# Low parts of the heads' weights made by an accumulating DMA from GpSimd, and weights split three pieces ahead

## The chip, the cores and the metric

The kernel runs on one core of a Trainium2 chip. The metric is the device time of one execution in microseconds: 1679.33 us is the median of three runs of the kernel before (1678.99 to 1681.47). The core's engines are TensorE (PE, with its weight loads PEld), VectorE (DVE), ScalarE (ACT), GpSimd (POOL) and SyncE (SP), which issues most of the transfers.

## What is computed

The reference is one decoder layer with two branches on 512 tokens of width 2048, all in float32: an attention with forgetting gates (8 heads of 128) and an RWKV-7 recurrence (16 heads of 64), each gated, then merged and projected.

```python
h = _rmsnorm(x, norm_gain)
u = h @ w_in
u_fox, u_rwkv, g_a, g_b = _split(u, (FOX_COLS, RWKV_COLS, D_MODEL, D_MODEL))
q, k, v, z_a, f_logit = _split(u_fox, FOX_SIZES)
o_a = _fox_attention(heads(q), heads(k), heads(v), log_f) * jax.nn.silu(z_a)
r, kr, vr, z_b, w_down, a_down = _split(_token_shift(u_rwkv, rwkv_shift_mix), RWKV_SIZES)
...
y = _rwkv7_scan(rh, heads(decay), kh, vh, kk, kk * ah)
o_b = (y + bonus) * jax.nn.silu(z_b)
m = jax.nn.sigmoid(g_a) * (o_a @ w_proj_fox) + jax.nn.sigmoid(g_b) * (o_b @ w_proj_rwkv)
return _rmsnorm(x + m @ w_out, final_norm_gain)
```

Per step, the scan is `S = S * w + sa * b + v * k` with `sa = S @ (-kk)`; the kernel computes it in eight chunks of 64 tokens for each pair of heads.

## The kernel before

**Three products for one.** Every large product is made of three: the activations are held as `hhi` and `hlo`, a high part that TensorE's fp32r format holds exactly and the rest, and each weight tile is split in the same way into `whi` and `wlo`. A product is then hhi·whi + hlo·whi + hhi·wlo, three matmuls of 128x128 by 128x512 into one accumulator (`product`, L295).

**Pieces.** The weights come in pieces of 256 KB: 128 partitions of four blocks of 128 columns, 12 matmuls each; a tile of 128 output columns has four of them (`_0`, `_4`, `_8`, `_12` in the names). `load_raw` (L253) lets SyncE load a piece into one of `RAWS` = 4 raw buffers. `split_pieces` (L271) makes the two parts: ScalarE copies raw to `whi` with rounding (L283) and VectorE subtracts, raw − whi, to `wlo` (L284). `whi` and `wlo` have four buffers each. `next_piece` (L259) is called when the program comes to a piece i: it issues loads up to piece i+4, splits up to piece i+2, and hands out piece i.

**Stages.** First, the norm, the transposes and two small tiles (`wd`, `ad`). Then the heads' tiles in turn: RWKV head pairs 0 and 1 (tiles k, r, z, v), then a FoX head (tiles fq, fk, fv, fz) and a head pair alternately. From about 950 us on, the gates and projections (pieces named g and p) and the product with `w_out` (o, `raw_o`). The matmuls of the heads' own work are gathered between the large products of the tiles that come later.

**A head pair** goes through: *front* (`rwkv_front`, from L510: the decay `tz`, the rate `a`, the key `kn`, the products `EK` and `AR`, the sums of `rkk`), *back* (`rwkv_back`, L629: a triangular system solved by 31 steps `Wt`, `W` on VectorE, then the small products `gp` and `dp` with the copies `GP`, half of them on ScalarE and half on VectorE, L703, and `DT`), *chain* (`rwkv_chain`, L717: in each of eight chunks `z`, its copy `zt`, `sa`, its copy `AV`, `st`, the new state `SV`; ScalarE also makes `pre` for it; each copy is made half by VectorE and half by ScalarE), and the *end* (`yv`, normalisation of `y`, and a GpSimd store `ob_d`, L796). A FoX head ends with a GpSimd store `oa_d` (L859).

**What sets the order.** The order of TensorE and SyncE is the order of the program, which a small planner makes: `clock[0]` adds up the matmuls' estimated times, and a head's next step runs when its due time by the table `LAG` has come. On VectorE, ScalarE and GpSimd a scheduler orders by priority: chain steps stand highest (`HP` = 300, with `HV` = 300), then the splits (`HW` = 150), then the FoX steps (`HF` = 100). Each engine executes its row in order, so a waiting instruction holds up those behind it.

Of the kernel before, what the change touches and what calls it, by code (L numbers as in the profile page):

```python
# [9 lines left out]
F32 = mybir.dt.float32  # L10
F32R = mybir.dt.float32r
AF = mybir.ActivationFunctionType
ALU = mybir.AluOpType
# [43 lines left out]
def hybrid_layer(  # L57
# [7 lines left out]
    V, S, G, PE = nc.vector, nc.scalar, nc.gpsimd, nc.tensor  # L65
# [187 lines left out]
    def load_raw(name, srcs, nk, M):  # L253
        raw = wpool.tile([P, nk, M], F32, tag="raw", bufs=RAWS, name=f"raw_{name}")
        for off, src in srcs:
            nc.sync.dma_start(raw[:, :, off:off + src.shape[1]], src.rearrange("(k p) m -> p k m", p=P))
        return raw

    def next_piece():  # L259


        i = used[0]
        used[0] += 1
        while len(raws) < min(i + (RAWS + 1 if i > 3 else 4), len(pieces)):
            raws.append(load_raw(*pieces[len(raws)]))
        split_pieces(i + (3 if i > 3 else 1))
        got = parts[i]
        parts[i] = None
        return got

    def split_pieces(n):  # L271
        while len(parts) < min(n, len(pieces)):
            j = len(parts)
            name, srcs, nk, M = pieces[j]
            raw = raws[j]
            whi = wpool.tile([P, nk, M], F32R, tag="whi", bufs=4, name=f"whi_{name}")
            wlo = wpool.tile([P, nk, M], F32R, tag="wlo", bufs=4, name=f"wlo_{name}")
            if j < 4:
                G.tensor_copy(whi, raw)
                G.tensor_tensor(wlo, raw, whi.bitcast(F32), ALU.subtract)  # L280
            else:
                with tc.high_priority(offset=HW):
                    S.activation(whi, raw, AF.Copy)  # L283
                    V.tensor_tensor(wlo, raw, whi.bitcast(F32), ALU.subtract)  # L284
            parts.append((whi, wlo))


# [7 lines left out]
    def product(ps, name, hi, lo):  # L295

        M, nk = spec[name]
        for k0 in range(0, nk, HK):
            whi, wlo = next_piece()
            for k in range(HK):  # L300
                kk = k0 + k
                mm(ps[0:M, :], whi[:, k, :], hi(kk), start=(kk == 0), stop=False)
                yield
                mm(ps[0:M, :], whi[:, k, :], lo(kk), start=False, stop=False)
                yield
                mm(ps[0:M, :], wlo[:, k, :], hi(kk), start=False, stop=(kk == nk - 1))
                yield
# [55 lines left out]
    for hf in range(2):  # L363
        t = slice(256 * hf, 256 * hf + 256)
        for j in range(0, KC + AHEAD, 2):
            if j < KC:
                turn(hf, j)
            if hf == 0 and j % 4 == 0 and j < KC:
                wd_w.append(next_piece())
                if j == 0:  # L370
                    for tb in range(2, 4):
                        for h2 in range(2):
                            load_x(nc.sync, tb, h2)
                    load_params()
            if hf == 0 and j in (SQ2, SQ3):
                norm_rows(2 if j == SQ2 else 3)
            if j < AHEAD:
                continue
            for kk in range(j - AHEAD, j - AHEAD + 2):
                whi, wlo = wd_w[kk // 4]  # L380
                mm(ps_wd[0:MW, t], whi[:, kk % 4, :], hhi[:, kk, t], start=(kk == 0), stop=False)
                mm(ps_wd[0:MW, t], whi[:, kk % 4, :], hlo[:, kk, t], start=False, stop=False)
                mm(ps_wd[0:MW, t], wlo[:, kk % 4, :], hhi[:, kk, t], start=False, stop=(kk == KC - 1))
            if hf == 1 and j - AHEAD in (4, 8, 12):
                split_pieces(4 + (j - AHEAD) // 4)
# [643 lines left out]
    for n in range(4):  # L1029
        pss = banks(n)  # L1030
        for kk in range(KC if n < 3 else KC // 2):
            whi, wlo = next_piece()
            if n == 1 and kk % 2 == 0:
                load_late(KC // 2 + kk // 2)
            for t in range(4):
                out_mm(pss[t], t, kk, whi[:, 0, :], wlo[:, 0, :])
        if n == 3:
            break
        for t in range(4):
            residual(pss[t], t, n)  # L1040
# [47 lines left out]
```

## Time and profile before

| | us |
|---|---|
| median of three runs | 1679.33 |
| the profiled execution's own time | 1682.03 |
| its span | 1680.3 |
| TensorE busy | 1632.0 (97%) |
| VectorE busy | 956.2 (57%) |
| ScalarE busy | 712.2 (42%) |
| GpSimd busy | 82.7 (5%) |

Times in the profile are microseconds from the start of the span. A row of the timeline gives an instruction's start, its duration, engine, line, operation and tiles; in brackets the idle time ahead of it on its engine and what ended that. A group row gives the busy time, the mean in nanoseconds of one, and the idle time ahead with its releasers. Transfers issued by GpSimd, `ob_d` for one, stand in GpSimd's row with the time that their issue takes, and are not counted as busy. The waits view adds up, for each engine, how long it waited for what.

### The profile page before, as it was taken

What the parts mean: (1) busy time and instruction counts of PE and PEld (TensorE: products, weight loads), DVE (VectorE), ACT (ScalarE), POOL (GpSimd) and SP (SyncE); (2) the same over time, 40 slices, a digit from 0 to 9 for tenths busy, and PEclk for the clock granted to TensorE, in tenths of its full rate; (3) what the DMA queues carried; (4) which work ended last, traced back from release to release, by engine and by line L of the source; (5) the groups of instructions that cost most, each with busy time, mean ns of one, the idle gap of its engine ahead of it and who ended that gap; (6) DMA issues with size and microseconds to landing.
All of it is one profiled execution on the core that took longest, in us unless ns stands there. A gap on an engine that the chain in (4) does not pass through costs nothing.

```text
span 1680.3 us, 23444 instructions
## 1 busy us (share of the span) xinstructions
PE 1632.0 (97%) x8506; PEld 1333.1 (79%) x8506; DVE 956.2 (57%) x2005; ACT 712.2 (42%) x1455; POOL 82.7 (5%) x149
## 2 busy tenths in 40 slices
PE   6999998989999989999999999999999999999998
PEld 6887876868778868888788787888888888888886
DVE  6469587795976867778768354222234333353432
ACT  7544455373464454554644444222223222243322
POOL 3000000010000000010000000000000000001110
PEclk9999999999999999999999999999999999999999
DMA  5342423333333423424334234335334333343422
GB/s 166 97 105 70 118 67 89 98 80 85 84 85 94 102 76 85 111 66 114 87 90 110 75 107 126 97 98 144 97 98 145 99 96 95 98 157 122 136 84 100
DMA packets 287978, 170.24 MB, mean 101 GB/s; under 512 B 38790, under 2 KB 270830, under 8 KB 287222
## 3 DMA queue, kind: packets, MB, share of 16 engines
q1 hardware_dynamic: 284358, 156.13, 35.2%
q0 software_dynamic: 2064, 9.46, 1.5%
q10 hardware_dynamic: 1440, 3.15, 0.5%
q8 instruction: 67, 1.10, 0.3%
q14 instruction: 49, 0.40, 0.1%
HBM read 158.19 MB, written 10.50 MB: 100 GB/s over the span
## 4 chain that ended last, share of the span: by engine, by line
PE 87%; DVE 8%; ACT 3%; issue 2%; DMA 1%; SPq 0%; POOL 0%; DVEq 0%; ACTq 0%; POOLq 0%
PE u_g L152 21%; PE o L152 10%; PE p L152 10%; PE u_fk L152 5%; PE u_fq L152 5%; PE u_v L152 5%; PE u_fz L152 5%; PE u_fv L152 4%; PE u_r L152 4%; PE u_z L152 4%; PE u_k L152 4%; DVE Wt L499 2%; PE fo L152 1%; DVE W L675 1%; PE sc L152 1%
## 5 line engine op out<-in xcount | busy, mean ns | idle before, releaser
L152 PE MATMUL u_g<-hhi,whi_g 128*128 128x512 f32 x512 | 200.4, 391 | 0.0
L152 PE MATMUL u_g<-hhi,wlo_g 128*128 128x512 f32 x512 | 200.2, 391 | 0.0
L152 PE MATMUL u_g<-hlo,whi_g 128*128 128x512 f32 x512 | 199.6, 390 | 0.0
L284 DVE TENSOR_TENSOR wlo_g<-raw_g,whi_g 128x512 fp32r<-128x512 f32 x128 | 88.3, 690 | 165.2 <-ACT whi_g L283 163.1
L283 ACT ACTIVATE whi_g<-raw_g 128x512 fp32r<-128x512 f32 x128 | 80.8, 632 | 223.3 <-PE u_g L152 115.9
L152 PEld LDWEIGHTS u_g<-hhi,wlo_g 128*128 128x128 f32 x512 | 96.1, 188 | 20.4
L152 PEld LDWEIGHTS u_g<-hlo,whi_g 128*128 128x128 f32 x512 | 96.1, 188 | 20.2
L152 PEld LDWEIGHTS u_g<-hhi,whi_g 128*128 128x128 f32 x512 | 96.1, 188 | 20.0
L499 DVE TENSOR_TENSOR Wt<-W,Lt 128x16 f32<-128x16 f32 (+30 forms) x248 | 102.4, 413 | 5.5
L284 DVE TENSOR_TENSOR wlo_p<-raw_p,whi_p 128x512 fp32r<-128x512 f32 x64 | 44.3, 692 | 102.0 <-ACT whi_p L283 102.0
L152 PE MATMUL p<-ohi,whi_p 128*128 128x512 f32 x256 | 101.2, 395 | 0.1
L152 PE MATMUL p<-olo,whi_p 128*128 128x512 f32 x256 | 100.2, 391 | 0.5 <-DVE olo L929 0.5
L152 PE MATMUL p<-ohi,wlo_p 128*128 128x512 f32 x256 | 100.4, 392 | 0.0
L283 ACT ACTIVATE whi_p<-raw_p 128x512 fp32r<-128x512 f32 x64 | 40.4, 631 | 122.9 <-PE u_g L152 118.8
L152 PE MATMUL o<-whi_o,mhi 128*128 128x512 f32 x224 | 87.3, 390 | 0.1
L152 PE MATMUL o<-whi_o,mlo 128*128 128x512 f32 x224 | 87.2, 389 | 0.0
L152 PE MATMUL o<-wlo_o,mhi 128*128 128x512 f32 x224 | 87.1, 389 | 0.0
L284 DVE TENSOR_TENSOR wlo_o<-raw_o,whi_o 128x512 fp32r<-128x512 f32 x56 | 42.6, 761 | 76.1 <-ACT whi_o L283 75.9
L675 DVE TENSOR_REDUCE W<-Wt 128x8 f32<-128x16 f32 (+30 forms) x248 | 72.1, 291 | 5.0
L283 ACT ACTIVATE whi_o<-raw_o 128x512 fp32r<-128x512 f32 x56 | 35.3, 631 | 83.5 <-PE o L152 78.5
L744 ACT ACTIVATE pre<-SV,E 64x64 f32<-64x64 f32 x112 | 38.6, 345 | 57.3 <-DVE SV L757 56.5
L152 PEld LDWEIGHTS p<-olo,whi_p 128*128 128x128 f32 x256 | 48.0, 188 | 12.6 <-DVE olo L929 2.1
(353 smaller groups left out, 3937.3 us busy)
## 6 DMA issues: line engine op xcount, KB each, us to landing
raw_g<-in_w_in_dram SPq DMA_DIRECT2D x128, 256.0 KB
raw_o<-in_w_out_dram SPq DMA_DIRECT2D x56, 256.0 KB
raw_k<-in_w_in_dram SPq DMA_DIRECT2D x32, 256.0 KB
raw_r<-in_w_in_dram SPq DMA_DIRECT2D x32, 256.0 KB
raw_z<-in_w_in_dram SPq DMA_DIRECT2D x32, 256.0 KB
raw_v<-in_w_in_dram SPq DMA_DIRECT2D x32, 256.0 KB
raw_fq<-in_w_in_dram SPq DMA_DIRECT2D x32, 256.0 KB
raw_fk<-in_w_in_dram SPq DMA_DIRECT2D x32, 256.0 KB
```

The lines of the kernel that those rows point to most:

```text
L152: PE.matmul(out, lhsT=lhsT, rhs=rhs, start=start, stop=stop, **kw)
L283: S.activation(whi, raw, AF.Copy)
L284: V.tensor_tensor(wlo, raw, whi.bitcast(F32), ALU.subtract)
L499: eng.tensor_tensor(o, a, b, op)
L675: V.tensor_reduce(W[:, :, i], tmp[:, :, 0:i + 1], AX.X, ALU.add)
L744: S.activation(pre[hs[q]], SV[hs[q], c, q, :], AF.Copy, scale=E1[hs[q], c, CH:CH + 1])
```

## The change

For all pieces of the heads' tiles (names beginning with k, r, z, v or f; 256 pieces) `wlo` is no longer made by VectorE. ScalarE writes the negated, rounded raw piece into `wlo`, so that this holds −whi, and a DMA issued by GpSimd adds the raw piece onto it in SBUF. `whi` is made by ScalarE as before. The pieces of `wd`, `ad`, `g`, `p` and `o` keep VectorE's subtraction. Besides, from the ninth piece on the splits run up to piece i+3 in place of i+2. The lines behind the change are five higher than before.

```diff
@@ next_piece
-        split_pieces(i + (3 if i > 3 else 1))
+        split_pieces(i + (4 if i > 7 else 3 if i > 3 else 1))
@@ split_pieces
                 with tc.high_priority(offset=HW):
+                    if name[0] in "krzvf":
+
+                        S.activation(wlo, raw, AF.Copy, scale=-1.0)
+                        G.dma_start(wlo.bitcast(F32), raw, accum_op=ALU.add)
                     S.activation(whi, raw, AF.Copy)
-                    V.tensor_tensor(wlo, raw, whi.bitcast(F32), ALU.subtract)
+                    if name[0] not in "krzvf":
+                        V.tensor_tensor(wlo, raw, whi.bitcast(F32), ALU.subtract)
```

The rows of TensorE and SyncE stand in the same order as before. On the others the order changes as follows (in a name, the numbers behind the tile are the head, the chunk or the piece, and a running number of the buffer).

ScalarE in the chain of head pair 0, first two chunks, before and then after; the weights split there are those of tile k of head pair 2:

```order
L740 COPY zt_0_1868<-z_0_0_1866 64x64
L283 ACTIVATE whi_k2_4_1920<-raw_k2_4_1853 128x512
L750 COPY AV_0_1845<-sa_0_0_1889 64x64
L283 ACTIVATE whi_k2_8_1953<-raw_k2_8_1879 128x512
L744 ACTIVATE pre_0_1930<-SV_0_1069,E1_0_483 64x64 x2
L740 COPY zt_0_1927<-z_0_1_1925 64x64
L283 ACTIVATE whi_k2_12_1977<-raw_k2_12_1918 128x512
L750 COPY AV_0_1845<-sa_0_1_1942 64x64
```

```order
L745 COPY zt_0_1921<-z_0_0_1919 64x64
L287 ACTIVATE whi_k2_4_1934<-raw_k2_4_1905 128x512
L285 ACTIVATE wlo_k2_4_1935<-raw_k2_4_1905 128x512
L755 COPY AV_0_1897<-sa_0_0_1943 64x64
L287 ACTIVATE whi_k2_8_1974<-raw_k2_8_1932 128x512
L749 ACTIVATE pre_0_1985<-SV_0_1096,E1_0_483 64x64 x2
L285 ACTIVATE wlo_k2_8_1975<-raw_k2_8_1932 128x512
L745 COPY zt_0_1982<-z_0_1_1980 64x64
L287 ACTIVATE whi_k2_12_2008<-raw_k2_12_1972 128x512
L755 COPY AV_0_1897<-sa_0_1_1997 64x64
L285 ACTIVATE wlo_k2_12_2009<-raw_k2_12_1972 128x512
```

Beside each `whi` there is now a negation to `wlo`, ahead of `AV`, ahead of the second `zt` and behind the second `AV`.

VectorE ahead of the copy `GP` of head pair 2, before and then after; `kn`, `tz`, `EK`, `AR`, `z` and `rkk` belong to the front of head pair 3:

```order
L284 TENSOR_TENSOR wlo_v3_12_3766<-raw_v3_12_3702,whi_v3_12_3765 128x512
L538 SCALAR_TENSOR_TENSOR tz_3_3660<-reset_531,tz_3_3660 128x512
L499 TENSOR_TENSOR EK_3_3665<-EK_3_3665,k_3_3427 128x512
L557 RECIPROCAL kn_3_3676<-kn_3_3676 128x128
L499 TENSOR_TENSOR AR_3_3684<-r_3_3550,E1_1_484 128x8x64
L284 TENSOR_TENSOR wlo_fq2_0_3808<-raw_fq2_0_3725,whi_fq2_0_3807 128x512
L559 SCALAR_TENSOR_TENSOR kn_3_3676<-k_3_3427,par_448,kn_3_3676 128x512
L567 SCALAR_TENSOR_TENSOR rkk_3_3688<-r_3_3550,par_448,EK_3_3665 128x512
L562 SCALAR_TENSOR_TENSOR AR_3_3684<-kn_3_3676,E1_1_484 128x8x64
L465 SCALAR_TENSOR_TENSOR z_3_3720<-u_z3_3554,par1m_452,z_3_3720 128x511
L443 TENSOR_TENSOR rlo_3_3691<-rkk_3_3688,rhi_3_3690 128x512
L703 COPY GP_2_3755<-gp_2_3738 32x256
```

```order
L543 SCALAR_TENSOR_TENSOR tz_3_3758<-reset_531,tz_3_3758 128x512
L562 RECIPROCAL kn_3_3774<-kn_3_3774 128x128
L564 SCALAR_TENSOR_TENSOR kn_3_3774<-k_3_3518,par_448,kn_3_3774 128x512
L504 TENSOR_TENSOR AR_3_3782<-r_3_3645,E1_1_484 128x8x64
L567 SCALAR_TENSOR_TENSOR AR_3_3782<-kn_3_3774,E1_1_484 128x8x64
L504 TENSOR_TENSOR EK_3_3763<-EK_3_3763,k_3_3518 128x512
L470 SCALAR_TENSOR_TENSOR z_3_3819<-u_z3_3649,par1m_452,z_3_3819 128x511
L572 SCALAR_TENSOR_TENSOR rkk_3_3786<-r_3_3645,par_448,EK_3_3763 128x512
L708 COPY GP_2_3855<-gp_2_3838 32x256
L504 TENSOR_TENSOR BK_3_4003<-EK_3_3763 64x8x64
L448 TENSOR_TENSOR rlo_3_3789<-rkk_3_3786,rhi_3_3788 128x512
```

The subtractions (a third, `wlo_v3_8`, stands directly ahead of the rows shown of before) are gone, and `rlo` stands behind `GP`.

GpSimd around the store `ob_d` of head pair 2, before and then after; `a` and `kn` belong to the front of head pair 4:

```order
L730 COPY AV_3_4809<-SV_3_3975 64x8x64 x2
L796 DMA ob_d_559<-y_2_4435 128x512
L549 TENSOR_SCALAR a_4_4883<-a_4_4883 128x512
L499 TENSOR_TENSOR kn_4_4888<-kn_4_4888,a_4_4883 128x512
L859 DMA oa_d_558<-fz_2_3889 128x512
```

```order
L286 DMA wlo_k4_12_4611<-raw_k4_12_4580 128x512
L286 DMA wlo_r4_0_4638<-raw_r4_0_4608 128x512
L801 DMA ob_d_559<-y_2_4552 128x512
L286 DMA wlo_r4_4_4686<-raw_r4_4_4635 128x512
L286 DMA wlo_r4_8_4711<-raw_r4_8_4683 128x512
L286 DMA wlo_r4_12_4735<-raw_r4_12_4708 128x512
L286 DMA wlo_z4_0_4769<-raw_z4_0_4732 128x512
```

The transfers of the pieces now stand in GpSimd's row ahead of and behind the store, which itself stands between those of `r4_0` and `r4_4`.

## Rows read from the trace of the kernel before

**Rows 1.** The page's head and first part: busy time, share and instructions of each engine.

```profile
span 1680.3 us, 23444 instructions
PE 1632.0 (97%) x8506; PEld 1333.1 (79%) x8506; DVE 956.2 (57%) x2005; ACT 712.2 (42%) x1455; POOL 82.7 (5%) x149
```

**Rows 2.** The page's chain that ended last, share of the span by engine.

```profile
PE 87%; DVE 8%; ACT 3%; issue 2%; DMA 1%; SPq 0%; POOL 0%; DVEq 0%; ACTq 0%; POOLq 0%
```

**Rows 3.** What TensorE waited for: us in total, times, longest.

```profile
PE dp L152 <- DVE GP L703: 9.7, 2, 5.3
...
PE fpt L156 <- ACT tz L536: 4.5, 1, 4.5
PE yv L152 <- DVE ylo L443: 2.6, 4, 0.9
...
PE sa L152 <- ACT zt L740: 1.5, 2, 1.1
```

**Rows 4.** Windows: length; busy PE, PEld, DVE, ACT, POOL; clock; DMA share; GB/s.

```profile
46.00:960.00 914.00, 887.93 (x5118) 721.38 (x5117) 668.26 (x1520) 453.66 (x982) 44.72 (x61) 0.99 0.36 90
240.00:280.00 40.00, 33.51 (x176) 25.13 (x170) 35.82 (x59) 23.23 (x40) 5.27 (x6) 0.91 0.28 75
...
365.50:372.70 7.20, 7.20 (x61) 5.57 (x59) 7.20 (x11) 7.06 (x14) 1.59 (x1) 1.00 0.27 73
...
600.00:640.00 40.00, 36.50 (x219) 30.05 (x220) 24.52 (x50) 16.22 (x44) 1.86 (x2) 0.91 0.23 60
```

**Rows 5.** Groups of VectorE's subtractions from 46 to 990 us.

```profile
L284 DVE TENSOR_TENSOR wlo_fk<-raw_fk,whi_fk 128x512 fp32r<-128x512 f32 x32 | 22.4, 699 | 22.1 <-ACT whi_fk L283 21.9
...
L284 DVE TENSOR_TENSOR wlo_fq<-raw_fq,whi_fq 128x512 fp32r<-128x512 f32 x32 | 21.8, 680 | 11.0 <-ACT whi_fq L283 10.7
```

**Rows 6.** DMA issues by group: count, KB each, median us from issue to landing.

```profile
xo<-in_x_dram POOLq DMA_DIRECT2D x4, 1024.0 KB, 7.4
...
ob_d<-y POOLq DMA_DIRECT2D x8, 256.0 KB, 2.5
```

**Rows 7.** Timeline of TensorE and ScalarE in a stretch at full rate.

```profile
545.46 0.39 PE L152 MATMUL u_fv<-hhi,wlo_fv 128*128 128x512 f32 x1
...
545.66 0.63 ACT L283 ACTIVATE whi_fz<-raw_fz 128x512 fp32r<-128x512 f32 x1 [2.09 <-PE u_fv L152]
...
554.30 0.39 PE L152 MATMUL u_fz<-hhi,wlo_fz 128*128 128x512 f32 x1
```

**Rows 8.** Timeline of VectorE and TensorE, 253 to 260 us.

```profile
253.60 0.63 DVE L284 TENSOR_TENSOR wlo_fq<-raw_fq,whi_fq 128x512 fp32r<-128x512 f32 x1
...
259.29 0.69 PE L156 MATMUL fpt<-ident,pr 128*128 128x128 f32 x4 [4.47 <-ACT tz L536]
259.71 0.71 PE L152 MATMUL u_v<-hhi,wlo_v 128*128 128x512 f32 x1
```

**Rows 9.** Timeline of VectorE and TensorE, 366 to 378 us.

```profile
367.56 1.23 DVE L284 TENSOR_TENSOR wlo_v<-raw_v,whi_v 128x512 fp32r<-128x512 f32 x2
...
372.20 0.67 DVE L284 TENSOR_TENSOR wlo_fq<-raw_fq,whi_fq 128x512 fp32r<-128x512 f32 x1
...
376.28 0.69 DVE L443 TENSOR_TENSOR rlo<-rkk,rhi 128x512 fp32r<-128x512 f32 x1 [0.81 <-POOL kn L499]
...
377.49 0.74 PE L152 MATMUL dp<-DT,GP 32*32 32x32 f32 x20 [4.43 <-DVE GP L703]
```

**Rows 10.** Timeline of GpSimd, and TensorE's first use of `wlo_r4_4`.

```profile
83.73 0.61 POOL L549 TENSOR_SCALAR a<-a 128x512 f32<-128x512 f32 x1 [33.52 <-ACT EK L548]
...
458.93 0.55 POOL L796 DMA_DIRECT2D ob_d<-y  x1 [21.93 <-DVE y L795]
...
462.65 0.39 PE L152 MATMUL u_r<-hhi,wlo_r 128*128 128x512 f32 x1
...
720.81 2.89 POOL L549 TENSOR_SCALAR a<-a 128x512 f32<-128x512 f32 x1 [36.24 <-ACT EK L548]
```

## The prediction, made before the result was known

> **What bounds the kernel now.** I read the page's first part first: TensorE is busy 1632.0 of 1680.3 us, VectorE 956.2, ScalarE 712.2, GpSimd 82.7 [rows 1]. The chain of waits says the same: 87% of the path that ended last is TensorE, 8% VectorE, 3% ScalarE [rows 2]. So the change, which takes no matmul away and adds none, can only act on the 48.3 us in which TensorE stands (1680.3 − 1632.0), and on the clock it is granted. I then read whom TensorE waits for [rows 3]: VectorE's copy `GP` 9.7 us in two waits, ScalarE's `tz` 4.5 in one, VectorE's `ylo` 2.6 in four, ScalarE's `zt` 1.5 in two. No row there names `whi` or `wlo`: the weights' halves are never late, and the subtractions that the change takes away are felt only where other work queues behind them. From 46 to 960 us, where the heads are made, TensorE is busy 887.93 of 914.00 us, so 26.1 us of standing is all that can be had there; VectorE works 668.26 (73%) and ScalarE 453.66 (50%) [rows 4]. The clock is told by the same view: three windows of 40 us, at 240, 360 and 600 us, have a mean granted clock of 0.91, the first and the last shown [rows 4]. Each holds or directly follows one of the three long stalls (4.47, 4.43 and 5.3 us) [rows 3, 8, 9]. At the two levels of 2.4 and 1.2 GHz a mean of 0.91 over 40 us is (1 − 0.91) × 40 / 0.5 = 7.2 us at the lower one, 3.6 us of work lost each time; after the stall at 259 us one matmul of 128x512 takes 0.71 us where 0.39 is usual [rows 7, 8].
>
> **The change part by part.** It concerns 256 pieces (16 tiles' worth of k, r, z, v for eight head pairs and q, k, v, z for eight heads, of four pieces each).
>
> *VectorE loses 256 subtractions.* There are eight groups of about 32; the longest and the shortest mean are 699 and 680 ns [rows 5]. At 0.68 the 256 are 174 us, and VectorE falls from 668 to about 494 of 914 us (54%). What this saves on TensorE's path is read from the stalls one by one.
> Stall A (254.8 to 259.3 us): TensorE waits 4.47 us for `tz`, which ScalarE makes after `y` and `zt`, and `y` waits for a row of reciprocals on VectorE. Three subtractions stand among these (246.75, 251.39 and 253.60 us; the last is shown, 0.63 us) [rows 8]. Up to 1.9 us goes; against this the transpose copy of the turn and the new negations share ScalarE, where one more operation of 0.6 us comes before `tz`: 1.9 − 0.6 = 1.3 (0 to 1.9).
> Stall B (372.8 to 377.5): TensorE waits 4.43 us for `GP`. In VectorE's row before it stand two subtractions (1.23 us) and a third (0.67), 1.9 us; and the new order moves `rlo` behind `GP`, which takes away its 0.69 and the 0.81 that it waited for GpSimd's `kn`, 1.5 us [rows 9]. That is 3.4 us at most. But in this stretch ScalarE is as full as VectorE: 7.06 and 7.20 of 7.20 us [rows 4], and it is given a negation for each of the three pieces that are split there, 3 × 0.63 = 1.9 us [rows 7], while its `tz`, `EK` and `E` feed the same VectorE row. So I count the 1.5 in full, and of the other 1.9 that ScalarE largely pays back a quarter: 2.0 (1.5 to 3.4).
> The third stall (5.3 us, the longest of the `GP` row) has one subtraction ahead of it and one negation in its place: 0 (−0.6 to 0.6). Of the four waits for `ylo` I take half, 1.3 (0 to 2.6).
> Clock: I take it that the most shortened stall, B, falls to some 2.4 us and no longer brings the lower clock: waits of 1.5 us and less [rows 3] have no window of 0.91 about them. 3.6 us (0 to 10.8).
> Gain: 1.3 + 2.0 + 0 + 1.3 + 3.6 = 8.2 us; at most 1.9 + 3.4 + 0.6 + 2.6 + 10.8 = 19.3.
>
> *ScalarE gains 256 activations* of one 128x512 tile, the size of the present `whi` (0.63 us) [rows 7]: 161 us, from 454 to about 615 of 914 us (67%). Two costs. In the chain, the first order fence shows a negation beside each `whi`, between `zt`, `AV` and `pre`; ScalarE copies one half of `zt` and of `AV` in each of 64 chunks, and TensorE waits for both halves; it waited for `zt` only twice, 1.5 us in all [rows 3], so most copies have slack. An activation of 0.63 that happens to run when a copy becomes ready delays it 0.3 us on average; with 161/914 = 18% more occupation and 128 copies that is 128 × 0.18 × 0.3 = 6.9 us of delay, of which I let 1.0 pass (0 to 5). In the fronts, where ScalarE is already full, three or so negations add 1.9 us each; two of eight fronts make TensorE wait today (the `tz` and the `GP` of B) and are counted above; I add one more, 1.9 (0 to 15, rival 1). Cost: 2.9.
>
> *GpSimd gains 256 transfers and TensorE a wait for their landing.* The issue itself takes 0.55 us there [rows 10], 256 × 0.6 = 154 us on an engine that works 44.72 of 914. The order of TensorE and SyncE is row for row the same. What counts is the time from a free slot to the first matmul with that `wlo`. In a stretch at full rate ScalarE begins `whi_fz` at 545.66, released by TensorE, and the first matmul that reads this piece's `wlo` is at 554.30 [rows 7]: 8.64 us, three pieces and a quarter, which is also what the change's look-ahead gives with four buffers. ScalarE needs 2 × 0.63, handing over some 0.2; so 7.1 us are left for issue and landing. The trace holds no transfer from SBUF to SBUF and no accumulating one. The nearest rows are GpSimd's stores of 256 KB, 2.5 us to landing, and its 1024 KB loads, 7.4 [rows 6]. An accumulating one reads twice and writes once, so I take 3 to 5 us, nearer the 256 KB row, and it is hidden; cost 0. At full rate a piece takes 12 × 0.227 = 2.7 us (39 matmuls lie between 545.46 and 554.30 [rows 7]), over the whole stretch 914/260 = 3.5, so most pieces have more time than this one; I take 40 of 256 as at full rate. At the upper bound of 7.4 each of these would be 0.3 us late, 12 us. Queued behind each waiting transfer on GpSimd are the next one, the `a` and `kn` steps and the stores. The `ob_d` store of head pair 2 is issued at 458.93, after a wait for `y`, and the third order fence shows `wlo_r4_4` right behind it; TensorE reads that one from 462.65 on [rows 10], so issue and landing have 462.65 − 459.48 = 3.2 us, just what I take for them. I count 0 for this and for the seven like it (0 to 3).
> The raw buffer is now given back by the landing and not by VectorE, 2 to 4 us later; a 256 KB transfer lands in 2.5 us [rows 6], and the load is issued two pieces, 5.4 us, before ScalarE needs it: 0 (0 to 3).
>
> *What speaks against the landing.* GpSimd's `tensor_scalar` on one shape takes 0.61 us in one place and 2.89 in another, where VectorE is busy too; a store issued from GpSimd beside a busy VectorE takes the usual 0.55 [rows 10]. If the work behind a transfer were held up as that operation was, a landing would be 2.3 us longer, 5.3 to 7.3 us, at its upper end past the 7.1 that are left; this is the greater part of rival 2. The Trainium skill (SBUF — State Buffer, "SBUF: two separate sides") states this rule: a VectorE operation in a two-port mode shuts GpSimd out of the port pair that they share, and a DMA issued there gets its descriptors late. The trace agrees for the compute operation; of transfers no run here shows it yet. By the rule alone the sum would be rival 2's.
>
> *Sum.* 8.2 − 2.9 = 5.3 us. The profiled execution took 1682.03 us, so 1676.7; it lies 2.7 over the median of 1679.33, which gives **1674.0 us**, 0.3% faster. (A measurement of this kernel tells 0.2%, 3.4 us, from no change.)
>
> **The rivals.** *Rival 1, slower: ScalarE becomes the bound of the fronts.* In stretch B it is busy 7.06 of 7.20 us now [rows 4], and I take the fronts of the other pairs to be like it, since they run the same code. If each of the eight is 1.9 us later and no slack is left, that is 15.2, with up to 5 in the chain and one lower-clock spell more (3.6): 23.8 − 8.2 = 15.6 over, 1695; half of it gives 1687. It decides where a front's result has less slack than the three negations ahead of it. For it: A ends on a ScalarE result. Against: only two of eight fronts hold TensorE up, and one of them on VectorE. Chance 0.21.
> *Rival 2, slower: the transfer lands too late,* from 7.1 us on, or GpSimd's queue stands behind `ob_d` and `kn`. At 8.5 us each full-rate piece is 1.4 us late: 40 × 1.4 − 8.2 = 48 us over, 1727; at 7.4, 12 − 5.3 = 7 over, 1686. For it: two reads per write, one queue, and the 2.89 us of [rows 10]. Against: 2.5 us for 256 KB [rows 6]. Chance 0.13.
> *Rival 3, no change:* TensorE's stalls have their own sequence (`kn`, `EK`, reciprocals on a ScalarE as full as VectorE), VectorE's freed time is time that it waits anyway, and the clock falls as before: 8.2 − 3.6 − 2.9 = 1.7 us, 1677.6. Chance 0.20. That the change doesn't do what it says would be this too: VectorE's 256 rows are gone in the new order, so I give that nothing.
> *Forecast,* 1665 to 1675: 0.46.
>
> **How the numbers follow.** Faster 0.46; same 0.20; slower 0.21 + 0.13 = 0.34. The range: below it is bounded by the gain of 19.3 us, 1660; above, half of rival 2 (0.07) and the worst of rival 1 (0.06) are left out, 1698. The forecast's own range is 1664 to 1676.
>
> **What would show it.** In the profile after, VectorE between 46 and 960 us should have about 494 us and ScalarE 615. TensorE's wait for `GP` at 377 should be some 2 us shorter, that for `tz` 1.3, and the window from 360 to 400 us should have a clock of 1.00. A row of TensorE waiting for `wlo`, or for the new transfer, of more than 3 us in all makes the step on the landing wrong; landings over 7 us are rival 2. More waits for `zt`, `tz` or other ScalarE results, over 8 us in all, are rival 1. If the waits shrink but the end doesn't move, the clock term or rival 3 is what failed.

## The result, and the profile after

The changed kernel takes 1689.84 us (median of four runs, 1688.28 to 1690.14) against 1679.45 for the kernel before: a ratio of 1.0058 with a 95% interval of 1.0040 to 1.0075. It is 10.4 us slower, where 5.3 us faster was forecast.

The page after, its first part and the chain [rows 1, 2 are those of before]:

```profile
span 1688.1 us, 23977 instructions
...
PE 1638.7 (97%) x8506; PEld 1339.2 (79%) x8506; DVE 808.7 (48%) x1749; ACT 844.0 (50%) x1711; POOL 299.3 (18%) x405
...
PE 81%; DVE 9%; ACT 5%; DMA 3%; issue 2%; SPq 1%; ACTq 0%; DVEq 0%; POOLq 0%
```

The work moved as described: VectorE lost 147 us, ScalarE gained 132, GpSimd 217. (The issues on GpSimd are counted as busy here, other than said above: its instructions rise from 149 to 405, by the 256 transfers.) On the chain, transfers (DMA) went from 1% to 3% and ScalarE from 3% to 5%. What TensorE waited for (us in total, times, longest; L152 and L156 are TensorE's lines), to be held against [rows 3]:

```profile
PE dp L152 <- DVE GP L708: 7.0, 5, 4.7
...
PE fpt L156 <- ACT fpT L839: 3.5, 1, 3.5
PE dp L152 <- ACT GP L708: 3.2, 3, 1.4
PE yv L152 <- DVE ylo L448: 2.6, 3, 1.0
PE sa L152 <- ACT zt L745: 2.1, 4, 1.0
```

The wait for `tz` is gone, and no row has TensorE waiting for `wlo` or for the new transfer. New are the 3.5 us for `fpT` and ScalarE's half of `GP`. Windows, columns as in [rows 4]:

```profile
46.00:960.00 914.00, 886.49 (x5080) 720.57 (x5079) 525.84 (x1269) 576.12 (x1218) 250.01 (x304) 0.98 0.78 160
...
240.00:280.00 40.00, 37.17 (x218) 28.69 (x217) 25.43 (x40) 29.59 (x53) 12.07 (x14) 0.96 0.72 146
360.00:400.00 40.00, 37.58 (x253) 30.39 (x252) 23.09 (x46) 24.01 (x58) 10.51 (x12) 0.96 0.68 140
455.00:495.00 40.00, 35.94 (x214) 28.53 (x213) 18.86 (x41) 28.37 (x62) 10.44 (x11) 0.91 0.66 135
600.00:640.00 40.00, 37.91 (x221) 31.39 (x222) 17.55 (x41) 20.42 (x52) 10.01 (x11) 0.91 0.59 118
```

The third column from the right is the granted clock, the next the share of time in which the 16 DMA engines are busy: 0.78 where it was 0.36.

**Where the time went.** TensorE's rows stand in the same order in both kernels, so each can be set against its counterpart and the difference of their starts followed. The changed kernel is ahead by 3.0 us at 140 us, by 6.9 at 260 (the wait for `tz`, 4.47 us, is gone as a whole) and by 9.9 at 380 (the stall for `GP` is 2.7 us shorter). Then it falls back: 6.7 us between 460 and 480, 2.9 between 580 and 620, 4.4 between 700 and 720, 3.8 between 820 and 840, 17.8 in all, each in the front of a head pair, beside which stands the back of the pair before. These are the "four places" in what follows. From 850 us on nothing changes any more: +7.8 us, the difference of the two profiled spans.

The first of these falls, between 455 and 470 us, in rows of GpSimd, SyncE (SPq), ScalarE and TensorE of the changed kernel:

```profile
456.13 0.85 POOL L286 DMA_DIRECT2D wlo_z<-raw_z  x1 [3.38 <-ACT wlo_z L285]
...
462.73 0.37 SPq L256 DMA_DIRECT2D raw_v<-in_w_in_dram  x1
463.15 0.49 SPq L526 DMA_DIRECT2D lora<-in_rwkv_w_dram  x1
463.69 0.44 SPq L527 DMA_DIRECT2D lora<-in_rwkv_a_dram  x1
...
468.04 0.40 ACT L447 CAST lora_h<-lora 96x256 fp32r<-96x256 f32 x1 [5.32 <-DMA lora<-in_rwkv_a_dram]
...
469.33 0.90 PE L156 MATMUL fpt<-ident,pr 128*128 128x128 f32 x3 [3.52 <-ACT fpT L839]
469.88 0.78 PE L152 MATMUL u_z<-hhi,wlo_z 128*128 128x512 f32 x1
```

The view of the tile `wlo_z` in this stretch gives the three landings there, from issue, as

```profile
DMA to landing us min/median/max: 4.9/5.1/6.5
```

The same place before, which is 9 us later in the time of its own span:

```profile
465.22 0.37 SPq L256 DMA_DIRECT2D raw_v<-in_w_in_dram  x1
...
467.12 0.42 SPq L522 DMA_DIRECT2D lora<-in_rwkv_a_dram  x1
...
469.08 0.41 ACT L442 CAST lora_h<-lora 96x256 fp32r<-96x256 f32 x1 [2.00 <-DMA lora<-in_rwkv_a_dram]
```

The transfer onto `wlo_z_0` is issued at 456.13. SyncE's next load, `raw_v`, needs the raw buffer that this transfer reads, and goes out at 462.73. Behind it in SyncE's row stand the two small `lora` loads. Set against TensorE's row, `raw_v` is 6.5 us later than before (462.73 + 9.0 − 465.22) and `lora` 5.6. ScalarE, whose row has `lora_h` ahead of `pr` and `fpT`, stands 5.32 us in place of 2.00, TensorE stands 3.52, and its next matmul of 512 columns takes 0.78 us: the lower clock, and with it the 0.91 of the window at 455 us. The small loads also take longer: from the issue of the second `lora` load to `lora_h` 4.35 us in place of 1.96 (468.04 − 463.69, 469.08 − 467.12).

The other small transfers in SyncE's row are those of a back: `w_d` writes VectorE's solution `W` out, and `W<-w_d` and `DT` read it back in another layout; VectorE then waits for the second. Over the heads' stage VectorE waited for it (in `A`, its first step on it) and ScalarE for `lora`, before and then after:

```profile
DVE A L691 <- DMA W<-w_d: 3.5, 3, 1.6
...
ACT lora_h L442 <- DMA lora<-in_rwkv_a_dram: 6.7, 4, 2.0
```

```profile
DVE A L696 <- DMA W<-w_d: 27.3, 9, 6.1
...
ACT lora_h L447 <- DMA lora<-in_rwkv_a_dram: 11.5, 3, 5.8
```

Four of the nine waits of VectorE, of 6.05, 3.25, 2.14 and 4.81 us, end at 453, 583, 699 and 816 us, each just ahead of one of the four places. At the third, a raw piece comes late itself:

```profile
702.92 0.63 ACT L285 ACTIVATE wlo_z<-raw_z 128x512 fp32r<-128x512 f32 x1 [5.31 <-DMA raw_z<-in_w_in_dram]
```

Its load stands in SyncE's row behind `w_d`, `W` and `DT`.

### The profile page after: what moved, and what is told of

The parts are those of the page before. It is cut to its first block, busy times and chain, and to the rows that moved or that the text cites. A ratio compares the mean times of both kernels' runs of the same rounds, so it can differ in the third digit from the quotient of the medians.

```text
span 1688.1 us, 23977 instructions
## 1 busy us (share of the span) xinstructions
PE 1638.7 (97%) x8506; PEld 1339.2 (79%) x8506; DVE 808.7 (48%) x1749; ACT 844.0 (50%) x1711; POOL 299.3 (18%) x405
## 4 chain that ended last, share of the span: by engine, by line
PE 81%; DVE 9%; ACT 5%; DMA 3%; issue 2%; SPq 1%; ACTq 0%; DVEq 0%; POOLq 0%
PE u_g L152 21%; PE o L152 10%; PE p L152 10%; PE u_fk L152 5%; PE u_fq L152 5%; PE u_v L152 5%; PE u_fz L152 4%; PE u_fv L152 3%; PE u_z L152 3%; PE u_k L152 3%; DVE Wt L504 3%; DVE W L680 2%; PE u_r L152 2%; PE fo L152 1%; PE sc L152 1%
## 5 line engine op out<-in xcount | busy, mean ns | idle before, releaser
L152 PE MATMUL u_g<-hhi,whi_g 128*128 128x512 f32 x512 | 200.4, 391 | 0.0
L152 PE MATMUL u_g<-hhi,wlo_g 128*128 128x512 f32 x512 | 200.2, 391 | 0.0
L152 PE MATMUL u_g<-hlo,whi_g 128*128 128x512 f32 x512 | 199.6, 390 | 0.0
L152 PEld LDWEIGHTS u_g<-hhi,wlo_g 128*128 128x128 f32 x512 | 96.1, 188 | 20.4
L152 PEld LDWEIGHTS u_g<-hlo,whi_g 128*128 128x128 f32 x512 | 96.2, 188 | 20.2
L152 PEld LDWEIGHTS u_g<-hhi,whi_g 128*128 128x128 f32 x512 | 96.1, 188 | 19.9
L152 PE MATMUL p<-ohi,whi_p 128*128 128x512 f32 x256 | 101.1, 395 | 0.0
L152 PE MATMUL p<-olo,whi_p 128*128 128x512 f32 x256 | 100.2, 391 | 0.5 <-DVE olo L934 0.5
L152 PE MATMUL p<-ohi,wlo_p 128*128 128x512 f32 x256 | 100.4, 392 | 0.0
L152 PE MATMUL o<-whi_o,mhi 128*128 128x512 f32 x224 | 87.3, 390 | 0.1
L152 PE MATMUL o<-wlo_o,mhi 128*128 128x512 f32 x224 | 87.2, 389 | 0.0
L152 PE MATMUL o<-whi_o,mlo 128*128 128x512 f32 x224 | 87.1, 389 | 0.0
L152 PEld LDWEIGHTS p<-olo,whi_p 128*128 128x128 f32 x256 | 48.1, 188 | 12.7 <-DVE olo L934 2.1
```

What stands on the lines that cost most here:

```text
L152: PE.matmul(out, lhsT=lhsT, rhs=rhs, start=start, stop=stop, **kw)
```

## The experiments

Three theories. **Q**: the accumulating transfer gives its raw buffer back late, SyncE's queue stands at the next raw load, and what stands behind it (`lora`, `w_d`) comes too late. **A**: ScalarE is overloaded (rival 1). **S**: the DMA engines are so busy that small transfers are slow by themselves. In what follows the ratio is to the kernel before on the same chip. All runs keep TensorE's row order. The plain copy keeps the order on every other engine too; the other edits also move some rows of VectorE and ScalarE (with both early about 50 of 1749 and 40 of 1675), an effect that no run takes apart from the edit itself.

**Loads one piece later.**

```diff
-        while len(raws) < min(i + (RAWS + 1 if i > 3 else 4), len(pieces)):
+        while len(raws) < min(i + (RAWS if i > 7 else RAWS + 1 if i > 3 else 4), len(pieces)):
```

> The changed kernel with SyncE's loads of raw pieces issued one piece later (up to piece i+3 in place of i+4), so that the small transfers behind them in SyncE's row (w_d, lora) stand behind one load fewer that waits for a landing. Theory Q (the accumulating transfer gives a raw buffer back some 5 us later, SyncE's queue stands at the next load, and w_d and lora behind it come too late for the front and the back of a head pair): w_d is issued about one piece, 2.7 to 3.5 us, sooner than the 9 to 12 us after the substitution's end that the changed kernel shows, and 5 to 10 us of the loss come back: 1680 to 1685. Theory A (ScalarE's 161 us of negations make the fronts late): 1690, no change. Theory S (the small transfers are slow because the 16 DMA engines are busy 78% of the time): 1690.

1.0057 (1.0041 to 1.0074): not the gain that Q had put down. `w_d` does go out 3.2 us sooner after the substitution's end, 7.6 us in place of 10.8 in the mean of head pairs 2 to 6. But now the raw pieces themselves come late. What ScalarE waited for in this kernel:

```profile
ACT whi_r L287 <- DMA raw_r<-in_w_in_dram: 16.0, 7, 4.3
...
ACT lora_h L447 <- DMA lora<-in_rwkv_a_dram: 10.4, 4, 4.8
```

In the changed kernel these are 7.6 and 11.5. The lateness was moved from one row of the same queue to another; this run alone decides nothing.

**Who does the new work.** The addition on VectorE, with ScalarE's negation kept:

```diff
-                        G.dma_start(wlo.bitcast(F32), raw, accum_op=ALU.add)
+                        V.tensor_tensor(wlo, raw, wlo.bitcast(F32), ALU.add)
```

> The changed kernel with the accumulating DMA replaced by VectorE: ScalarE negates as in the change, VectorE adds the raw piece, so ScalarE has all the new work, VectorE the old amount, and the raw buffers come back from VectorE. Theory Q: the loss of 17.8 us after 430 us is gone, and the gain of 9.9 us before it too, since VectorE is as full as before: about 1680 (1678 to 1685). Theory A: the loss stays and the gain is gone: 1695 to 1700. Theory S: about 1680.

1.0018 (1.0009 to 1.0028). The negation on VectorE, with the transfer kept:

```diff
-                        S.activation(wlo, raw, AF.Copy, scale=-1.0)
+                        V.tensor_scalar(wlo, raw, -1.0, None, ALU.mult)
```

> The changed kernel with the negation made by VectorE (a multiplication by -1) in place of ScalarE; the accumulating DMA stays. ScalarE's work is back at 454 us in the heads' stage, VectorE gains 256 times 0.4 us or so. Theory Q: SyncE's queue is as late as in the changed kernel, w_d 9 us and more behind the substitution: 1685 to 1692. Theory A: ScalarE is relieved, 1672 to 1680. Theory S: 1685 to 1692.

1.0137 (1.0111 to 1.0162). The windows of the two, from 46 to 970 us:

```profile
46.00:970.00 924.00, 896.93 (x5149) 729.59 (x5148) 674.50 (x1527) 585.34 (x1236) 44.95 (x61) 0.99 0.35 90
```

```profile
46.00:970.00 924.00, 884.32 (x5061) 718.31 (x5059) 603.75 (x1507) 449.47 (x969) 248.89 (x302) 0.98 0.77 157
```

With all of ScalarE's new work (585 us) and no transfer the kernel is within 0.2% of before; with ScalarE relieved (449 us) and the transfer kept it is the slowest of all. Set against TensorE's rows, the first loses 3.5 us at the four places, the second 18.3, as much as the changed kernel (17.8). The loss goes with the transfer and not with ScalarE's negations: theory A falls. In the second kernel ScalarE stands longer for transfers than in any other:

```profile
ACT lora_h L447 <- DMA lora<-in_rwkv_a_dram: 20.3, 6, 6.0
ACT whi_z L287 <- DMA raw_z<-in_w_in_dram: 18.0, 8, 5.1
```

It is slower still than the changed kernel because the gain up to 400 us is missing (2.9 us behind there, where the changed kernel is 9.8 ahead). Why wasn't separated: VectorE is not relieved, it makes the negation late besides, and TensorE waits 4.6 us for the transfers themselves.

**The look-ahead alone**, in the kernel before:

```diff
-        split_pieces(i + (3 if i > 3 else 1))
+        split_pieces(i + (4 if i > 7 else 3 if i > 3 else 1))
```

> The kernel before with only the look-ahead of the change (splits up to piece i+3), subtraction on VectorE. All theories: no part of the loss, 1679.5 within 3 us, because before the change ScalarE already began a split as soon as a buffer was free.

1.0009 (0.9999 to 1.0018): no part of the loss that can be told from none.

**SyncE's small transfers earlier.** Two edits which leave TensorE's row order as it is. `lora` of the next pair is loaded at the end of a front:

```diff
-        lora = w("lora", (LORA, 2, P))
-        nc.sync.dma_start(lora[:, 0, :], rwkv_w2[0][:, p * P:(p + 1) * P])
-        nc.sync.dma_start(lora[:, 1, :], rwkv_a2[0][:, p * P:(p + 1) * P])
+        if p not in loras:
+            load_lora(p)
+        lora = loras.pop(p)
...
         free["rk"] = p
+        if p + 1 < NP:
+            load_lora(p + 1)
```

and `w_d`, `W`, `DT` are issued 8 us of planned time earlier (`EARLY` = 8):

```diff
-        yield LAG["sub"]
+        t0 = clock[0]
+        yield LAG["sub"] - EARLY
         w_d = dram.tile([32, 4, 256], F32, tag="w_d", bufs=2, name=f"w_d_{p}")
...
+        yield t0 + LAG["sub"] - clock[0]
         A1 = w("Wt", (P, NC, 32), n="A1")
```

> The changed kernel with one edit: the two small lora loads of a head pair stand in SyncE's row right behind the front of the pair before, some 100 us earlier; TensorE's order is the same row for row. Theory Q (SyncE's queue stands behind the landing of the accumulating transfers, and what stands behind the raw loads comes too late): ScalarE's 11.5 us of waiting for lora and TensorE's 3.5 us stall at 469 us go, with the lower clock behind it: 4 to 7 us less than the changed kernel, that is 0.1 to 0.3% over the kernel before. Theory S (the small transfers are slow by themselves, the DMA engines being busy 78% of the time): the same gain, since the loads have 100 us; this run does not tell Q from S, it prices the lora part.

1.0026 (1.0014 to 1.0039): about 5 us better than the changed kernel, as expected. The stall at 469 us is gone; the ones for `GP` stay. (The profiled execution is the slowest of ten, 1691.44 us where the median is 1686.68.)

> The changed kernel with one edit: the transfers w_d, W and DT stand in SyncE's row 8 us of planned time earlier (two or three raw loads ahead), everything on TensorE at its old place. Theory Q: w_d is issued within 4 us of the end of the substitution in place of 9 to 12, VectorE's wait for W (27.3 us) falls below 8, TensorE's waits for GP (10.2 us) fall to about half, and 5 to 9 us come back: 0 to 0.3% over the kernel before. Theory S: w_d is issued earlier but takes as long as it did, and the gain is the same only if it lands earlier; its own time from issue to the next load, 3.7 to 6.2 us in the changed kernel against 3.0 to 4.2 before, stays at 4 to 6.

1.0079 (1.0058 to 1.0100): worse, against the expectation. `w_d` goes out 0 to 3.6 us behind the substitution, but it now stands ahead of `lora` and of raw loads, and ScalarE's wait for `lora` rises:

```profile
ACT lora_h L448 <- DMA lora<-in_rwkv_a_dram: 25.4, 6, 5.7
```

That is 25.4 us where the changed kernel has 11.5. One row of a late queue was served at the expense of the next. `w_d` itself still takes 4.9 us from the first of its four issues to the load behind it (mean of head pairs 2 to 6), 5.0 in the changed kernel and 3.5 before, as theory S had it.

> Both edits. Theory Q: what the change gained up to 400 us (9.9 us) stays, most of the 17.8 us lost later comes back: 10 to 16 us less than the changed kernel, so 0 to 0.4% faster than the kernel before. If ScalarE's negations or the transfers themselves were the cause (theories A, S), not over 4 us come back.

0.9967 (0.9956 to 0.9979), 1676.91 us: 0.33% faster than the kernel before, some 15 us better than the changed kernel, with the same matmuls, negations and transfers. TensorE's main waits, and the window of the first fall:

```profile
PE dp L153 <- DVE GP L721: 7.3, 2, 4.4
...
PE yv L153 <- DVE ylo L449: 2.6, 3, 1.0
PE sa L153 <- ACT zt L758: 2.5, 5, 1.0
...
PE u_r L153 <- DMA wlo_r<-raw_r: 2.2, 1, 2.2
```

```profile
455.00:495.00 40.00, 39.62 (x241) 31.58 (x241) 22.00 (x45) 33.24 (x73) 12.52 (x14) 1.00 0.77 152
```

At the four places nothing is lost any more; ahead of them the gain is smaller, 6.0 us at 400 us and not 9.8. So the way of the loss is shown: it runs through `lora` and `w_d`. But Q and S are not told apart by it. A transfer that is issued early hides a late place in the queue and a slow transfer alike, and here `w_d` goes out 7.1 us earlier than even in the kernel before. The transfers are still slow: the DMA engines are as busy as in the changed kernel (0.77 in this window), and `w_d` takes 4.7 us to the load behind it.

> The two edits in the kernel before the change, as a control. Its w_d is issued 0 to 3 us behind the substitution and ScalarE waits 6.7 us for lora in all: 0 to 3 us less than the kernel before by every theory. If it gains as much as the changed kernel does by them, the late queue is no effect of the change.

1.0038 (1.0026 to 1.0050): slower. In the kernel before the substitution ends later, so the early `w_d` waits for it and holds the raw loads behind it; TensorE waits 4.6 us for `whi_fv` at 180 us. The edits are no improvement in themselves; in the changed kernel, where the substitution ends earlier and the queue is later, they are one.

**A late queue without the change.**

```diff
-        raw = wpool.tile([P, nk, M], F32, tag="raw", bufs=RAWS, name=f"raw_{name}")
+        raw = wpool.tile([P, nk, M], F32, tag="raw", bufs=3, name=f"raw_{name}")
```

> The kernel before the change with three raw buffers in place of four, nothing else: no accumulating transfer, ScalarE and VectorE work as before, the orders of TensorE and SyncE are the same row for row, and each raw load waits for a piece one nearer. Theory Q: this alone makes SyncE's queue one piece (2.7 to 3.5 us) later, w_d is issued 3 to 6 us behind the substitution in place of 0 to 3, and the time rises by 3 to 12 us (0.2 to 0.7%). Theories A and S, in which the negations or the traffic of the DMA engines cost the time: within 0.1% of the kernel before.

1.0021 (1.0011 to 1.0030). The raw buffers alone move the time in the direction and, just, by the size that Q gave. A and S have nothing to act on here: `w_d` takes 3.5 us to the load behind it, as before. But the price speaks against Q by itself. `w_d` and `lora` go out as late as in the changed kernel (3.3 and 2.6 us, there 2.0 and 3.5), and at the four places that costs 2.7 us and not 17.8; the greater part, 4.1 us, is lost ahead of 140 us, where the changed kernel loses nothing. In the kernel before, at least, a late issue alone does not make the loss.

**The addition itself.**

```diff
-                        G.dma_start(wlo.bitcast(F32), raw, accum_op=ALU.add)
+                        G.dma_start(wlo.bitcast(F32), raw)
```

> The changed kernel with the transfer a plain copy from SBUF to SBUF: the addition is left out (the low parts hold the weights themselves), everything else stands. It prices the addition. If the addition is what makes the landing long, the plain copy lands in 2.5 us where the accumulating one takes 4.0, the DMA engines are busy some 55% in place of 78%, and w_d is issued 1.5 us sooner; if the length is the descriptors' work on GpSimd, it lands in 4 us as well.

One run: 1673.69 us, beside 1681.94 for the kernel before. Groups of transfers, the last number the median time from issue to landing, of the changed kernel and of this one:

```profile
wlo_k<-raw_k POOLq DMA_DIRECT2D x32, 256.0 KB, 4.3
...
wlo_v<-raw_v POOLq DMA_DIRECT2D x32, 256.0 KB, 3.8
```

```profile
wlo_k<-raw_k POOLq DMA_DIRECT2D x32, 256.0 KB, 2.8
...
wlo_v<-raw_v POOLq DMA_DIRECT2D x32, 256.0 KB, 2.5
```

Its window of the heads' stage, with the DMA share at 0.56:

```profile
46.00:970.00 924.00, 903.50 (x5206) 737.15 (x5205) 530.65 (x1287) 592.02 (x1251) 176.23 (x313) 0.99 0.56 162
```

The addition makes a landing about 1.3 us longer and takes the DMA engines from 56% to 78%. With the rows of every engine in the same order that turns 0.5% faster (one run) into 0.6% slower; at the four places the plain copy loses 5.5 us in place of 17.8. The transfer's addition is what costs the time. It makes the raw buffers come back later and the other transfers slower at once (`w_d` takes 4.4 us and not 5.0), so this run too does not tell Q from S.

**Two variants of the best version.** `w_d` of head pair 0 at its old place (`EARLY if p else 0.0`):

> As both_early, but w_d of head pair 0 at its old place: there the early w_d waits for the substitution's end and holds the raw loads behind it. TensorE's loss of 2.3 us between 140 and 160 us goes if that is its cause: 0 to 3 us less than both_early, 0.3 to 0.5% faster than the kernel before. If it stays, its cause is VectorE's order around 146 us and not SyncE's queue.

0.9982 (0.9971 to 0.9993). The 2.2 us at 146 us stay, so the early `w_d` is not their cause. TensorE waits there for VectorE's `z`; the kernel with `lora` alone early has the same wait and that with `w_d` alone early has not, and VectorE's row is in another order there than in the changed kernel, which is the likely cause. The variant is not better. And the look-ahead taken back, `split_pieces(i + (3 if i > 3 else 1))`:

> The changed kernel with lora and w_d early, and the change's look-ahead taken back (splits up to piece i+2). If the look-ahead is needed for the landing (4.0 us and more of the 7.1 left, of which one piece, 2.7 us, goes), TensorE waits for the accumulating transfers, over 5 us in all, and the time is 5 to 15 us over both_early. If ScalarE starts a split when a buffer is free whatever the look-ahead, it is the same as both_early within 3 us, or 1.5 us better by what the look-ahead alone cost in the kernel before.

0.9995 (0.9985 to 1.0004): 0.3% behind the version with it. TensorE waits 1.9 us for the transfers, no longer than with the look-ahead (2.2), so in this profile the landing is not what the look-ahead is needed for. The profiled execution is the fastest of ten, though (1677.22 us, 1.0 behind the other's, where the median is 1681.25), and what the look-ahead is needed for stays open.

**Eight of the kernels in one table.** "Late" is how much later than in the kernel before the first `w_d` (mean of head pairs 2 to 6) and `lora` (mean of all eight) go out, set against the TensorE row that starts at that moment in the kernel before. The third column is the sum of all waits of ScalarE for transfers from 46 to 960 us.

| kernel | `w_d` late, us | `lora` late, us | ScalarE waits for transfers, us | ratio |
|---|---|---|---|---|
| before | 0 | 0 | 15.3 | 1 |
| addition on VectorE | 0.0 | 0.2 | 10.1 | 1.0018 |
| three raw buffers, before | 3.3 | 2.6 | 21.5 | 1.0021 |
| changed | 2.0 | 3.5 | 41.2 | 1.0058 |
| changed, plain copy | 0.6 | 1.8 | 18.5 | 0.995 (one run) |
| changed, negation on VectorE | 3.2 | 3.7 | 67.7 | 1.0137 |
| changed, loads later | −1.3 | 0.4 | 53.7 | 1.0057 |
| changed, both early | −7.1 | early | 37.1 | 0.9967 |

The ratio does not follow any one column: the kernel with three raw buffers has `w_d` later than the changed one and a third of its loss. Of the last kernel's 37.1 us, 5.0 are for `lora` and 31.3 for raw pieces; between 430 and 850 us its longest wait is 3.4 us, where the changed kernel has two of 5.3.

## Why the prediction was wrong

**The step that failed** is one sentence: "The raw buffer is now given back by the landing and not by VectorE, 2 to 4 us later; a 256 KB transfer lands in 2.5 us [rows 6], and the load is issued two pieces, 5.4 us, before ScalarE needs it: 0 (0 to 3)." Its lateness was about right in the mean (`lora` goes out 3.5 us late), and too small at the first of the four places (6.5 for `raw_v`). Its error is that it follows only the raw load and not SyncE's queue: a load that waits for its buffer holds up what stands behind it, and there stand `lora`, `w_d`, `W` and `DT`, which have deadlines of their own. The prediction did ask who is queued behind a waiting instruction for GpSimd, and not for SyncE, whose wait the change lengthened. Nor did it ask what 256 more transfers do to the pace of the others. Its term was 0 to 3 us. Measured is 17.8 us lost at the four places, 5.5 with the plain copy, none with `lora` and `w_d` issued early; in the median the kernel with both early is 15 us better, which is no pure price of the term, since `w_d` is there ahead of its old place.

**Rival 2** had the cause in the wrong place: the landing is late for SyncE, not for TensorE, which waits for no `wlo`. The landing was well sized: 3 to 5 us, measured 3.8 to 4.3 in the median of a group, up to 6.5 in the stretch shown. That it was hidden from TensorE was right.

**Rival 1** and the 2.9 us of ScalarE's cost: the run with the addition on VectorE prices the negation with the look-ahead at 0.18%, 3.0 us, with no relief of VectorE beside it. So the term of 2.9 us came out near; how much of it falls to the chain and how much to the fronts, the two parts it was made of, wasn't measured. Rival 1's time, 1687 to 1695, was hit by luck, with another cause. Even its sign could mislead: TensorE's waits that end on ScalarE add up to 16.4 us, 11.2 before, but at the first and third place ScalarE itself stood for a transfer, and with ScalarE relieved of the negations the loss at the four places is the same. The 161 us were too many: ScalarE's busy time rose by 122 us from 46 to 960 us (453.66 to 576.12) and by 132 in the whole execution, since neighbouring activations of 0.63 us overlap by about 0.1 (two of them start at 455.22 and 455.74). VectorE fell to 526 and not to 494, I take it for the same reason: durations of single rows add up to more than the engine's time.

**The gains** were larger than forecast, up to 400 us: stall A 4.5 us and not 1.3, B 2.7 and not 2.0, and two waits for the low-rank weights at 129 to 131 us, 2.5 us together, were not counted at all; `ylo` gave nothing (2.6 us, as before). What went wrong with A: I counted the three subtractions shown in the row ahead of it, but VectorE's whole row runs earlier: the substitution ends 5 to 10 us earlier against TensorE in pairs 0 to 6. With the addition on VectorE, which is then as full as before, the wait for `tz` is back at 3.3 us. I take from it that an engine that is 73% full gives back what it saved since it last stood idle, and not only what it saved in the stretch looked at.

**The clock.** The window at 360 us has 0.96 and not 1.00: the shorter stall halved the spell at the lower level and did not end it. Over the whole stage, adding (1 − clock) × 40 / 0.5 over the windows of 40 us, the lower level was held 24.8 us before, 34.4 after and 13.6 with both early. At half the work that is 12.4, 17.2 and 6.8 us lost. Of the 7.8 us by which the span grew, 4.8 are the clock's; of the 5.8 by which it shrank with both early, 5.6. So a long stall counts about twice: the 3.52 us at 469 us bring a window at 0.91, that is 3.6 us of work more. That is what makes a late small load dear.

**The rule of the Trainium skill** that the prediction weighed (SBUF — State Buffer, "SBUF: two separate sides"): GpSimd's transfers were not held up beside a busy VectorE to any extent that shows in the medians. The plain copies, issued in the same places, land in 2.5 to 3.0 us, near the 2.5 of the stores before [rows 6]; what lengthens the accumulating ones goes with the addition. Single copies took up to 5.6 us; why, wasn't looked into, and the trace does not tell which of VectorE's operations run in the two-port mode that the rule speaks of.

**What stays open.** Whether the small transfers come too late by their place in SyncE's queue (Q) or by moving slowly beside the accumulating ones (S): the changed kernel has both. Even a store that has nothing to do with the weights lands later there, in 4.1 us, than the 2.5 of before, and it stands between the new transfers in GpSimd's row, so that here too place and slowness are mixed:

```profile
ob_d<-y POOLq DMA_DIRECT2D x8, 256.0 KB, 4.1
```

And the interplay: lateness of the issue alone costs the kernel before 0.2%, the negation 0.2%, and the changed kernel lost 17.8 us. That ScalarE, while it stands for `lora`, also holds up the negations behind it, and these the transfers and the next raw buffers, fits the rows between 455 and 470 us, but was not tried apart. Nor were more raw buffers tried.

## What to carry to other kernels

When a buffer is given back later, follow the queue of whoever waits for it, and list what stands behind that wait with its own deadline; a large load that may wait and a small one that may not do not belong in one queue in that order. After relieving an engine, look at what its results still have to pass through: here VectorE was 5 to 10 us earlier and its result lay waiting for SyncE. Moving one late row ahead served it at the expense of the next; both had to move. And ask what many new transfers do to the pace of the small ones beside them.

## What was not expected of the hardware

An accumulating transfer of 256 KB within SBUF lands in 3.8 to 4.3 us where a plain one takes 2.5 to 3.0, and at the same bytes moved per second (159 and 162 GB/s) the 16 DMA engines are busy 78% of the time in place of 56%. Its issue on GpSimd takes 0.85 us, that of the plain copy in the same place 0.54 and that of the stores 0.55 [rows 10].
